# A down projection with sixteen of its 22 row tiles as seven block products

## The chip, the cores and the metric

The kernel runs on one core of one Trainium2 chip. The metric is the device time of one execution in microseconds, as the median of several runs. The engines are TensorE (PE: matmuls; PEld are its weight loads), VectorE (DVE), ScalarE (ACT), GpSimd (POOL) and SyncE (SP), whose queue issues most of the transfers.

## What is computed

A transformer block: modulation and norm, an input projection, two mixers (a chunkwise mLSTM and a block attention), a gated merge, and a gated feed-forward part. The end is what matters here (512 tokens, D = 1024, D_FF = 2816, all in float32):

```python
h = modulate(rms_norm(x, norm2_g[l]), sh2, sc2)
f = silu(h @ w_gate) * (h @ w_up)          # 512 x 2816
x = x + g2[:, None, :] * (f @ w_down)      # 2816 x 1024
return rms_norm(x, normf_g)
```

## The kernel before, in words

Every large matmul is made of float32r parts. A float32 operand is rounded to a "hi" part (ACT, line 207 for weights, 230 in `split` for activations) and the remainder "lo" is formed by a subtraction (DVE, lines 209 and 231). `mm3` (lines 223 to 227) then issues three matmuls: hi x hi, hi x lo, lo x hi.

Weights come in chunks of up to 128 x 2048 elements (1 MB). `load` issues a chunk's transfer on SP's queue into one of four `raw` tiles; `cvt` splits half a chunk into two of the four `whl` slots. `begin(n)` issues loads two and three chunks ahead and splits the first half of chunk n+1, `mid(n)` its second half. So a chunk's split can start only when the chunk two before it has been used up by PE and has given its slots back. The order on every engine is the order of the program; each engine works its own queue in order and waits on semaphores.

The feed-forward part has 22 gate and up chunks of 256 columns (C_GU to C_DN-1). From chunk FIRST = C_GU+3 to LAST, `seven` (line 1481) forms each by seven block products instead of eight; the block sums are made on DVE. The result f stands transposed in 22 tiles `ft[k]` of 128 rows by 512 tokens: the first sixteen in the pool `hp` (sixteen 128x512 tiles), the last six in the pool `xp`. Meanwhile the residual x is put aside in DRAM (`xkeep`, line 1591) and fetched back into `t` tiles before the down projection (line 1613). POOL forms the row sums of the gate g2 (`ada_sum`, lines 274 and 277) in the background of this stage, in bursts, on weights that use the same four `raw` tiles.

The down projection (lines 1619 to 1645) keeps eight PSUM banks open, one for each of four token blocks i and two column halves q. w_down comes in eleven chunks of 256 rows by 1024 columns. `gate_weights` (line 183) multiplies a chunk by the row g2 on DVE, four 128x512 operations for each chunk, so that PSUM holds the gated product. For each of the 22 k tiles, 4 x 2 `mm3` follow, that is 24 matmuls of 128x512; the stationary operand is f, the moving one is the weights. `fsplit(k+2)` splits the f tile two k tiles ahead. The last two chunks (four k tiles) are worked by `tail` in an order of banks that lets the last norm and the stores start early: first chunk NC-2 for a few banks ahead (`ahead_of`), then chunk NC-1 for one bank after the other, and `residual`, `root`, `close` and `scale` finish each token block.

## Time and profile before

| | |
|---|---|
| median of 3 runs | 775.61 us (775.3 to 776.21) |
| span of the profiled execution | 773.8 us |
| mean granted TensorE clock | 0.997 |
| instructions | 12047 |
| moved by DMA | 106.81 MB |

No time of the profiled execution other than its span is given, so the span stands for it. "Busy" is the time in which an engine executes; an operation's own duration includes a latency that the next one can overlap. A row of a group gives line, engine, operation, tiles written and read, shapes and count, then busy us, mean ns of one, and the idle time before it with what ended it. A row in order of time gives start, duration, engine, line, operation. Matmul rows overlap, so their rate is read from their starts.

### The profile page before, as it was taken

To read this page: it belongs to the slowest core of one execution; us is meant where nothing else is said; L and a number is where in the kernel's file an instruction comes from. 1 tells how busy PE (TensorE), PEld (TensorE's weight loads), DVE (VectorE), ACT (ScalarE), POOL (GpSimd) and SP (SyncE) were. 2 spreads that over 40 slices of the span, in tenths; PEclk is the share of its full clock that TensorE was granted. 3 is DMA by queue.
4 is the path that set the end of the run, shared out by engine and by line. 5 is a ranking of instruction groups with operands and counts; after the bars stand their busy time and mean duration, and the time that the engine had idled before them with its cause. 6 is when DMAs were issued, how large, how long until landed. Compare 5 with 4: busy or idle time off the path is not lost.

```text
span 773.8 us, 12047 instructions
## 1 busy us (share of the span) xinstructions
PE 762.4 (99%) x4635; PEld 665.3 (86%) x4635; DVE 543.9 (70%) x873; ACT 368.7 (48%) x656; POOL 328.2 (42%) x423
## 2 busy tenths in 40 slices
PE   8999999999999999999999999999999999999996
PEld 7789988778877877788889999999999998888885
DVE  5677877665575553388646789898999887754565
ACT  6679744323444553422347655545554543333143
POOL 5484535999875678980001108090835000000000
PEclk9999999999999999999999999999999999999998
DMA  9944325345421332327332522406053337422002
GB/s 333 389 167 179 110 81 161 106 169 218 163 111 55 110 118 109 155 97 284 109 109 89 178 75 91 183 25 231 32 219 152 122 114 240 135 84 108 1 1 108
DMA packets 25273, 106.81 MB, mean 138 GB/s; under 512 B 3704, under 2 KB 3840, under 8 KB 15616
## 3 DMA queue, kind: packets, MB, share of 16 engines
q1 hardware_dynamic: 23392, 103.62, 37.1%
q10 hardware_dynamic: 1824, 2.43, 1.2%
q8 instruction: 36, 0.59, 0.3%
q14 instruction: 21, 0.17, 0.1%
HBM read 99.74 MB, written 4.19 MB: 134 GB/s over the span
## 4 chain that ended last, share of the span: by engine, by line
PE 91%; DVE 5%; DMA 2%; ACT 1%; issue 1%; DVEq 0%; SPq 0%
PE psm L224 13%; PE psm L226 13%; PE psm L225 13%; PE psb L224 7%; PE psb L226 7%; PE psb L225 7%; PE psa L224 6%; PE psa L225 6%; PE psa L226 5%; PE psa L594 1%; DMA t<-in_dram 1%; PE psa L1095 1%; PE psc L1153 1%; PE psm L594 1%; PE psb L1136 1%; DVE whl L1452 1%
## 5 line engine op out<-in xcount | busy, mean ns | idle before, releaser
L209 DVE TENSOR_TENSOR whl<-raw,whl 128x1024 fp32r<-128x1024 f32 (+2 forms) x88 | 111.4, 1270 | 81.8 <-ACT whl L207 79.1
L207 ACT CAST whl<-raw 128x1024 fp32r<-128x1024 f32 (+2 forms) x87 | 88.5, 1033 | 104.1 <-PE psb L225 68.6
L277 POOL TENSOR_TENSOR accp<-accp,prod 128x256 f32<-128x256 f32 x112 | 97.9, 874 | 9.3
L274 POOL TENSOR_SCALAR prod<-ada,cact 128x256 f32<-128x256 f32 x112 | 93.0, 830 | 0.0
L1446 ACT CAST whl<-raw 128x1024 fp32r<-128x1024 f32 x57 | 59.8, 1049 | 69.0 <-DVE raw L1436 46.2
L1452 DVE TENSOR_TENSOR whl<-raw,whl 128x1024 fp32r<-128x1024 f32 x57 | 72.4, 1272 | 13.4 <-ACT whl L1446 13.2
L224 PE MATMUL psa<-t,whl 128*128 128x256 f32 x276 | 79.0, 286 | 0.9 <-DVE hs L1539 0.5
L226 PE MATMUL psa<-t,whl 128*128 128x256 f32 x276 | 78.1, 283 | 0.0
L225 PE MATMUL psa<-t,whl 128*128 128x256 f32 x276 | 78.1, 283 | 0.0
L224 PE MATMUL psm<-hh,whl 128*128 128x512 f32 x192 | 77.5, 404 | 0.5 <-ACT x L1077 0.5
L224 PE MATMUL psm<-t,whl 128*128 128x256 f32 (+1 forms) x256 | 76.1, 297 | 0.0
L225 PE MATMUL psm<-t,whl 128*128 128x256 f32 (+1 forms) x256 | 75.8, 296 | 0.0
L226 PE MATMUL psm<-t,whl 128*128 128x256 f32 (+1 forms) x256 | 75.8, 296 | 0.0
L226 PE MATMUL psm<-hh,whl 128*128 128x512 f32 x192 | 75.0, 390 | 0.0
L225 PE MATMUL psm<-hl,whl 128*128 128x512 f32 x192 | 74.9, 390 | 0.0
L1666 POOL TENSOR_TENSOR t<-t,t 128x512 f32<-128x512 f32 x1 | 1.3, 1293 | 170.2 <-DVE ss L1673 170.2
L224 PEld LDWEIGHTS psa<-t,whl 128*128 128x128 f32 x276 | 52.9, 192 | 1.6 <-DVE hs L1539 1.1
L225 PEld LDWEIGHTS psa<-t,whl 128*128 128x128 f32 x276 | 52.9, 192 | 0.1
L226 PEld LDWEIGHTS psa<-t,whl 128*128 128x128 f32 x276 | 52.9, 192 | 0.0
L225 PEld LDWEIGHTS psm<-t,whl 128*128 128x128 f32 x256 | 49.0, 191 | 1.3
L224 PEld LDWEIGHTS psm<-t,whl 128*128 128x128 f32 x256 | 49.0, 191 | 1.3
L226 PEld LDWEIGHTS psm<-t,whl 128*128 128x128 f32 x256 | 49.0, 191 | 1.3
(454 smaller groups left out, 2027.8 us busy)
## 6 DMA issues: line engine op xcount, KB each, us to landing
raw<-in_dram SPq DMA_DIRECT2D x59, 1024.0 KB, 4.8
ada<-in_dram SPq DMA_DIRECT2D x16, 1024.0 KB, 4.8
t<-in_dram SPq DMA_DIRECT2D x32, 256.0 KB, 6.0
raw<-in_dram SPq DMA_DIRECT2D x8, 448.0 KB, 6.3
xin<-in_dram SPq DMA_DIRECT2D x4, 512.0 KB, 5.5
t<-t ACTq DMA_DIRECT2D x32, 64.0 KB, 2.6
x<-in_dram SPq DMA_DIRECT2D x8, 256.0 KB, 7.0
xk<-x SPq DMA_DIRECT2D x8, 256.0 KB, 6.4
```

The costliest lines, as they stand in the source:

```text
L207: (eng.tensor_copy if eng else A.copy)(hi[:, s], raws[n][:, s])
L209: (eng or V).tensor_tensor(out=lo[:, s], in0=raws[n][:, s], in1=hi[:, s].bitcast(F32), op=ALU.subtract)
L224: PE.matmul(o, lh, rh, start=start, stop=False, skip_group_check=again)
L225: PE.matmul(o, lh, rl, start=False, stop=False, skip_group_check=again)
L226: PE.matmul(o, ll, rh, start=False, stop=stop, skip_group_check=again)
L274: G.tensor_scalar(t[:], rv[:, k, :], cact[:, k:k + 1], 1.0, op0=ALU.mult, op1=ALU.mult)
L277: G.tensor_tensor(out=p[:], in0=p[:], in1=t[:], op=ALU.add)
L594: PE.matmul(g1[m][:], w[:, blk(m)], h[:], start=k == 0 and e == 0, stop=k == KD - 1 and e == 2)
L1095: PE.matmul(bs[e][:, o:o + n], qp[a][r, blk(i)], kp[b][r, :n], start=g == 0, stop=g == 2)
L1136: PE.transpose(tb[:, o + (i - j) * 128:o + (i - j + 1) * 128], es[i][:, blk(j)], ident[:])
L1446: A.copy(hi, src)
L1452: V.tensor_tensor(out=lo, in0=src, in1=hi.bitcast(F32), op=ALU.subtract)
```

## The change

Sixteen k tiles (rows 512 to 2559 of w_down, `ft[4]` to `ft[19]`) leave the plain loop. They are taken as a product of 2 x 2 blocks: f in two token halves of 256 and two row halves of 1024, w_down in two row halves and two column halves of 512. Seven products (order 1, 2, 5, 6, 3, 7, 4) of 256 x 1024 by 1024 x 512 replace eight. Each product has two groups of four k tiles and two token blocks; its PSUM banks (`yb`, `xb2`, `zb`) hold on to partial results, which are copied out (`keep`) and combined later.

The four weight sums that the products need are formed in DRAM: POOL issues eight transfers of 2 MB (a copy, then an adding transfer, for each sum), the first two beside the merge projection (`next(wsums)` at ci = 0 and 2), the others before every third `seven`. `load` reads them as chunks. The f sums are formed in place in `ft`'s tiles, now four `hp` tiles of 128x2048: `sum3` on POOL, `sum1`, `sum2`, `sum4` on DVE. The products' weights are not gated by g2; `gated_sum` adds a kept tile to a PSUM bank on DVE, multiplies by g2 on POOL and adds to the residual on POOL. Three chunks stay plain (PLAIN: `ft` 0 to 3, 20, 21), of which the last two go to `tail`; the first one is gated on POOL. f's plain tiles are split one k tile ahead. The stores to `xkeep` move ahead of the first gate and up matmuls, and the first four f tiles lie in `xp`.

```diff
+PLAIN = (0, 1, 10)
...
-    for q in range(NF // 2):
+    for r in range(2):
+        for c in range(2):
+            for g in range(2):
+                got.append(("w_down", 512 + 1024 * r + 512 * g, 4, 512 * c, 512))
+    for q in PLAIN:
         got.append(("w_down", 256 * q, 2, 0, D))
...
+C_PL = 71
+PRODUCTS = (1, 2, 5, 6, 3, 7, 4)
...
-    hp = ctx.enter_context(tc.tile_pool(name="hp", bufs=16))
+    hp = ctx.enter_context(tc.tile_pool(name="hp", bufs=4))
...
+    def weight_sums():
+        for p, q, b in ((5, None, (0, 0)), (7, None, (1, 1)), (6, 7, (0, 0)), (4, 6, (1, 0))):
+            G.dma_start(wsum[p][:], wsum[q][:] if q else weight_block(0, 1), max_dma_last_dim=8192)
+            yield
+            G.dma_start(wsum[p][:], weight_block(*b), accum_op=ALU.add, max_dma_last_dim=8192)
+            yield
...
     xkeep = [dp.tile([128, D], F32, tag="xk", name=nm("xk")) for _ in range(NT)]
+    for i in range(NT):
+        for q in range(2):
+            SP.dma_start(xkeep[i][:, q * 512:q * 512 + 512], xr[i][q][:])
...
+    def aparts(t):
+        o, g, j = t // 4, t // 2 % 2, t % 2
+        b = {1: (0, 0), 2: (0, 1), 4: (1, 1), 7: (0, 0)}.get(PRODUCTS[o], (1, 0))
+        v = fblock(*b, g)[:, 2 * j:2 * j + 2, :]
+        ap[t] = tuple(T(dt=F32R)[:].rearrange("p (k t) -> p k t", k=2) for _ in range(2))
+        split(*ap[t], v)
+
+    def sum3(g, eng):
+        eng.tensor_tensor(out=fblock(0, 0, g), in0=fblock(0, 0, g), in1=fblock(1, 0, g), op=ALU.subtract)
...
     for n in range(FIRST, LAST + 1):
         if n == FIRST + 1:
             rows_free.append(1)
+        if (n - FIRST) % 3 == 0:
+            next(wsums, None)
         seven(n)
...
+    def gated_sum(name, banks, e, i, q, op):
+        t = kept[name][e]
+        V.tensor_tensor(out=t, in0=banks[e][:], in1=t, op=ALU.add)
+        G.tensor_tensor(out=t, in0=t, in1=g2row[q][:, :512], op=ALU.mult)
+        G.tensor_tensor(out=xr[i][q][:], in0=xr[i][q][:], in1=t, op=op)
...
+    hooks = {
+        (1, 0): lambda: sum3(1, G),
+        (2, 0): lambda: (keep("m1", yb, [W()[:, :512] for _ in range(2)]), sum1(0)),
+        (3, 0): lambda: sum1(1),
+        (4, 0): lambda: sum2(0),
+        (5, 0): lambda: sum2(1),
+        (6, 0): lambda: (keep("m5", zb, pair()), sum4(0)),
+        (7, 0): lambda: sum4(1),
+        (8, 0): lambda: keep("u2", yb, pair()),
+        (8, 1): lambda: gated_sum("m1", xb2, 0, 0, 0, ALU.add),
+        (9, 0): lambda: gated_sum("m1", xb2, 1, 1, 0, ALU.add),
+        (10, 0): lambda: gated_sum("u2", zb, 0, 0, 1, ALU.subtract),
+        (10, 1): lambda: gated_sum("u2", zb, 1, 1, 1, ALU.subtract),
+        (11, 1): lambda: gated_sum("m5", yb, 0, 2, 1, ALU.subtract),
+        (12, 0): lambda: (gated_sum("m5", yb, 1, 3, 1, ALU.subtract),
+                          gate_weights(C_PL, 0, G), gate_weights(C_PL, 1, G)),
+    }
+
+    groups = 2 * len(PRODUCTS)
+    for g in range(groups):
+        n = C_DN + g
+        p = PRODUCTS[g // 2]
+        for e in (2, 3):
+            load(n + e)
+        wh, wl = parts_of(n)
+        for e in range(2):
+            hooks.get((g, e), lambda: None)()
+            if g < groups - 1:
+                aparts(2 * g + 2 + e)
+            elif e == 0:
+                fps[0] = fsplit(0)
+            cvt(n + 1, e)
+            for k in range(4):
+                ah, al = (v[:, k % 2, blk(e)] for v in ap[2 * g + k // 2])
+                mm3(target[p][e][:], ah, al, wh[:, k, :], wl[:, k, :], p in (1, 2, 5) and g % 2 == 0 and k == 0,
+                    g % 2 == 1 and k == 3, True)
...
+    for e in range(2):
+        t = T()
+        V.tensor_tensor(out=t[:], in0=yb[e][:], in1=g2row[0][:, :512], op=ALU.mult)
+        G.tensor_tensor(out=xr[2 + e][0][:], in0=xr[2 + e][0][:], in1=t[:], op=ALU.add)
...
+    ch = begin(C_PL)
+    for kk in range(2):
+        if kk:
+            mid(C_PL)
+        fps[kk + 1] = fsplit(kk + 1)
...
+    last = [begin(C_PL + NP - 2)]
+    mid(C_PL + NP - 2)
+    last.append(begin(C_PL + NP - 1))
+    for k in range(3, 2 * NP):
+        fps[k] = fsplit(k)
```

## The prediction

> **What bounds the kernel now.** I read the page first (span, busy shares, chain), then the table by stage, then the groups and the order of time in the down projection.

> ```profile
> span 773.8 us, 12047 instructions
> PE 762.4 (99%) x4635; PEld 665.3 (86%) x4635; DVE 543.9 (70%) x873; ACT 368.7 (48%) x656; POOL 328.2 (42%) x423
> PE 91%; DVE 5%; DMA 2%; ACT 1%; issue 1%; DVEq 0%; SPq 0%
> ```

> TensorE is busy for 99% of the span and 91% of the chain that ended last runs through it. So a matmul taken away is worth its time, as long as nothing else becomes late. The table by stage says how much room the others have (columns: stretch, its length, then busy time and count of PE, PEld, DVE, ACT, POOL, then clock, DMA share, GB/s):

> ```profile
> 455.00:647.00 192.00, 191.14 (x1582) 190.30 (x1581) 173.32 (x240) 97.41 (x158) 72.69 (x60) 1.00 0.38 138
> 645.00:745.00 100.00, 99.87 (x449) 82.70 (x448) 60.90 (x84) 30.50 (x40) 0.00 (x0) 1.00 0.25 92
> 745.00:774.00 29.00, 22.32 (x110) 18.78 (x108) 17.46 (x47) 11.64 (x28) 1.29 (x1) 0.92 0.20 73
> ```

> The second row is the down projection: PE full, DVE at 61%, POOL idle. This is the stage that the change rebuilds. What one matmul costs there is read from the order of time: between these two rows lie one k tile's 24 matmuls.

> ```profile
> 739.81 0.39 PE L224 MATMUL psa<-whl,t 128*128 128x512 f32 x1
> ...
> 745.25 0.39 PE L224 MATMUL psa<-whl,t 128*128 128x512 f32 x1
> ```

> (745.25 - 739.81) / 24 = 0.2267 us each; the 0.39 is a latency, not a rate.

> **What goes.** Sixteen k tiles took 16 x 24 = 384 matmuls. Seven products of 2 token blocks x 8 k tiles x 3 parts are 336, of the same 128x512 form. 48 x 0.2267 = **10.9 us** less PE. Eight of eleven gated weight chunks also lose their four 128x512 multiplications on DVE. That ends a short stall just after the stage's start at 646.88, where PE's next start comes 0.52 instead of 0.23 us after the one before (a pause of 0.3):

> ```profile
> 646.88 0.40 PE L224 MATMUL psa<-whl,t 128*128 128x512 f32 x1
> ...
> 650.08 0.39 PE L226 MATMUL psm<-whl,t 128*128 128x512 f32 x1
> 650.60 0.50 PE L224 MATMUL psm<-whl,t 128*128 128x512 f32 x1
> ```

> **What is added beside PE.** The work is now 14 groups of 24 matmuls, 5.44 us each, and every group needs a whole new weight tile of 128x2048 rounded and subtracted; before, that fell on 48 matmuls, 10.9 us. The prices:

> ```profile
> L209 DVE TENSOR_TENSOR whl<-raw,whl 128x1024 fp32r<-128x1024 f32 x22 | 26.8, 1222 | 40.0 <-ACT whl L207 40.0
> L207 ACT CAST whl<-raw 128x1024 fp32r<-128x1024 f32 x22 | 23.0, 1049 | 72.0 <-PE psb L225 52.8 <-DVE raw L183 12.8 <-issue 6.3
> L231 DVE TENSOR_TENSOR t<-hs,t 128x512 fp32r<-128x512 f32 x16 | 11.0, 685 | 0.0
> L230 ACT CAST t<-hs 128x512 fp32r<-128x512 f32 x16 | 9.8, 615 | 0.0
> L1700 DVE SCALAR_TENSOR_TENSOR t<-t,ss,t 128x512 f32<-128x512 f32 x6 | 4.3, 749 | 0.1
> L1666 POOL TENSOR_TENSOR t<-t,t 128x512 f32<-128x512 f32 x1 | 1.3, 1293 | 170.2 <-DVE ss L1673 170.2
> ```

> These means hold some 0.09 us of latency; back to back DVE starts faster:

> ```profile
> 659.29 1.22 DVE L209 TENSOR_TENSOR whl<-raw,whl 128x1024 fp32r<-128x1024 f32 x1 [1.12 <-ACT whl L207]
> 660.44 1.29 DVE L183 TENSOR_TENSOR raw<-raw,v 128x512 f32<-128x512 f32 x2
> 661.64 0.68 DVE L231 TENSOR_TENSOR t<-hs,t 128x512 fp32r<-128x512 f32 x1
> 662.25 1.22 DVE L209 TENSOR_TENSOR whl<-raw,whl 128x1024 fp32r<-128x1024 f32 x1
> ```

> So 1.14 us for 1024 elements and 0.60 for 512; for ACT, the same way, 0.96 and 0.53. A group costs DVE 2 x 1.14 (weights) + 2 x 0.60 (f parts) = 3.5 us; in groups 2 to 7 an f sum of 1.14 to 1.24 comes on top: 4.7 of 5.44. ACT has 2 x 0.96 + 2 x 0.53 = 3.0. The weights of group n+1 can only be rounded when group n-1 has given its slots back, that is, from the start of group n, but then they need about 1.05 + 1.14 + 0.60 + 1.14 = 3.9 us of the 5.44. With DVE for itself, groups 0 to 13 keep PE full. I price them at zero, and DVE's 0.8 us of slack per group is the cover.

> **Where the cover goes.** POOL was idle here. Now it gets two 128x1024 subtractions (groups 0 and 1), then from group 8 six gated sums of two operations each, then the four multiplications that gate the first plain chunk, all 128x512 with both inputs in SBUF, and DVE runs the same kind. What the two do to each other stands in the old kernel's early stage:

> ```profile
> 77.22 1.23 DVE L209 TENSOR_TENSOR whl<-raw,whl 128x1024 fp32r<-128x1024 f32 x1 [1.23 <-ACT whl L207]
> 77.96 1.63 POOL L679 TENSOR_TENSOR t<-t,t 128x509 f32<-128x509 f32 x1 [1.21 <-ACT t L668]
> 78.37 1.77 DVE L647 SCALAR_TENSOR_TENSOR x<-t,t 128x512 f32<-128x512 f32 x1
> ```

> ```profile
> 558.19 1.59 POOL L277 TENSOR_TENSOR accp<-accp,prod 128x256 f32<-128x256 f32 x1
> 559.10 1.22 DVE L1452 TENSOR_TENSOR whl<-t,whl 128x512 fp32r<-128x512 f32 x1
> ```

> POOL's operation comes at 77.96, while DVE's is running; it gets on only when that ends (78.37), and DVE's next, which takes 0.749 alone (L1700), takes 1.77. They take turns, and POOL's waiting operation goes ahead of DVE's next. POOL ends at 79.59, 1.22 after its turn came; DVE ends 0.55 after that, so its turn began some 0.14 to 0.20 before POOL's end, and one POOL operation holds DVE up by 1.22 - 0.14 = **1.1 us**. The later pair of rows shows the same at half the size. [...]

> Laid on one time axis from the start of group 0 (group g at 5.44 g, the plain chunk at 76.2), each operation starting when its engine, its inputs, its slots and that access are free:
> First, groups 0 to 8: DVE has the slack for two double holds of 2.2; nothing is late.
> Second, groups 9 to 13. POOL's first gated sum comes at 47.5 (group 8 at 43.5, then 0.53 + 0.53 + 0.96 on ACT, 1.14 + 0.60 on DVE, 0.2 of latencies). Until the first half of the plain chunk's weights is ready, DVE still has 5 additions from PSUM at 0.60, 10 f remainders at 0.60 and 10 weight remainders at 1.14, 20.4 us. Ahead of it are 12 + 2 POOL operations; one of the 14 falls into a wait of DVE, 13 x 1.1 = 14.3. 47.5 + 20.4 + 14.3 = 82.2, against 76.2. Operation by operation, with ACT's waits, it is 82.5: PE is **6.3 us** late at the plain chunk.
> Third, the plain chunk's first half, 5.44 us of PE. From 82.5, DVE waits for POOL's last gate and ACT's rounding (1.1 + 0.2 + 1.05), then does the second weight half (1.14), two additions (1.2), two gates (1.2) with two more POOL operations between (2.2), waits for ACT (1.05), does a weight half (1.14), two gates (1.2), and only then the f remainder of k tile 1 (0.6): 82.5 + 12.1 = 94.6 (94.4 in the layout). PE wants that at 82.5 + 5.44 + 0.45 = 88.4. **6.1 us** with the half microsecond of latencies. Without POOL's turns both terms shrink to 0.7.
> Fourth, the tail. Before, f parts were split two k tiles ahead; now one ahead, so k tile 3 of the plain part is split after the last chunk's weights, whose slots come free when the plain chunk ends. Before, the same spot looked like this:

> ```profile
> 745.27 2.00 ACT L207 CAST whl<-raw 128x1024 fp32r<-128x1024 f32 x2 [6.33 <-issue]
> 746.36 2.36 DVE L209 TENSOR_TENSOR whl<-raw,whl 128x1024 fp32r<-128x1024 f32 x2 [4.91 <-ACT whl L207]
> 747.18 1.13 ACT L230 CAST t<-x 128x512 fp32r<-128x512 f32 x2
> 748.63 1.29 DVE L231 TENSOR_TENSOR t<-x,t 128x512 fp32r<-128x512 f32 x2
> ```

> There the first remainder was ready at 748.63 + 0.69 = 749.3, 4.1 us after the chunk's end at 745.25, and PE came to it then. Now PE wants it after 0.68 + 0.45 = 1.1: **3.0 us**, whatever POOL does.

> **The gate and up stage.** POOL issues eight 2 MB transfers from DRAM to DRAM, four of them adding. No row shows one. The nearest is 1 MB into SBUF in 4.8 us (the second row is for the stores below):

> ```profile
> raw<-in_dram SPq DMA_DIRECT2D x59, 1024.0 KB, 4.8
> ...
> xk<-x SPq DMA_DIRECT2D x8, 256.0 KB, 6.4
> ```

> The sums are needed stages later, so only others can suffer: weight loads that wait for POOL's row sums, and DVE behind them.

> ```profile
> SPq L163 <- POOL prod L274: 65.5, 4, 17.5
> ```

> ```profile
> DVE t L1431 <- DMA raw<-in_dram: 2.6, 3, 1.3
> ```

> Three loads already come late for DVE, yet DVE has 192 - 173 = 19 us free there. Below zero is excluded, since nothing is taken away; above, three loads later by a landing each, 3 x 4.8 = 14, less what DVE absorbs, about 6. I take **1.0**, nearest to the 2.6 now absorbed, range 0 to 6. [...] The eight stores to xkeep go ahead of one weight load on SP's queue, and the first f tiles wait for them; both have the second norm's projections as cover, and the larger tiles are given back with the same last readers: zero, at most one store's 6.4 us if the cover is gone.

> **Sum.** The profiled execution's span is 773.8; the median of the runs is 775.6, so 1.8 lie around it. 773.8 - 10.9 - 0.3 + 6.3 + 6.1 + 3.0 + 1.0 = 779.0, with 1.8 **780.8 us**, slower by 0.7%. Measurements of this kernel tell about 0.2% (1.6 us) from no change.

> **Rivals.** A: as above, 62%, 776 to 786 (the whole-instruction hold of 1.29 gives 784.1 and has some 10 of the 62; a DVE lead kept longer gives 776).
> B: POOL's operations do not hold DVE up in this stage, because they slip into DVE's waits for ACT (40.0 us before L209 in the old stage). Then the stall is 0.7 + 3.0: 775.6 - 10.9 - 0.3 + 3.7 + 1.0 = 769.1. For it speaks that idle time; against it, that DVE's load per time doubles and that idle time shrinks to 0.8 us per group. It decides where POOL's total hold from group 8 on, 16 x 1.1 = 18 us, fits DVE's gaps. 18%.
> C: half of the holds fall into gaps: laid out with 0.65 per hold, 8 us of stall: 773.3, range 771 to 777. 12%.
> D: the transfers starve the weight loads, at the far end, 6 instead of 1: 785.8 to 788. It takes over where a load lands over 3 us late in two of the bursts. 8%.
> That the matmuls saved are not saved can't be; their count and form are written out.

> Faster by over 0.2% (below 774.1): B and 7 of C's 12, 25%. Slower by over 0.2% (above 777.2): 55 of A, 8 of D, 63%. Same: 12%. The range for eight in ten, 769 to 787, cuts half of B and half of D; A's own is 776 to 786.

> **What would show it.** Right: PE full to about group 10, then pauses of PE that ACT's and DVE's weight groups end; POOL's 128x512 operations at some 1.9 to 2.4 us instead of 1.29 from group 8 on; L209 and L231 longer than 1.22 and 0.685 there; a wait of ACT's rounding for POOL's gates; a pause of 3 us just after the plain chunk, ended by an f remainder on DVE. The down projection still starts within 2 us of 646.88. Wrong: POOL rows near 1.3 with DVE rows unchanged (B), or PE waits before the down projection behind weight loads (D).

## The result, and the profile after

The changed kernel takes 786.94 us (median of four runs, 786.13 to 787.13), the kernel before 775.82 us beside it (775.3 to 776.21): a ratio of 1.0137, 95% interval 1.0125 to 1.015. It is slower, by 11.1 us, where the prediction had said slower by 5.2. The direction and the mechanism stand; the size is twice the forecast's.

First the page of the changed kernel: span, busy time of each engine, and the chain that ended last.

```profile
span 785.3 us, 12061 instructions
PE 761.3 (97%) x4587; PEld 660.2 (84%) x4587; DVE 576.5 (73%) x875; ACT 390.0 (50%) x686; POOL 370.0 (47%) x451
PE 84%; DVE 7%; DMA 4%; POOL 2%; issue 2%; ACT 1%; SPq 0%; ACTq 0%; POOLq 0%; DVEq 0%
```

The 48 matmuls are gone (4635 to 4587), but PE's busy time fell by only 1.1 us, not by 10.9. So something made the remaining matmuls longer, and PE's share of the chain fell from 91% to 84%. The table by stage shows where (columns: stretch, length, busy time and count of PE, PEld, DVE, ACT, POOL, then granted clock, DMA share, GB/s):

```profile
653.00:700.00 47.00, 46.70 (x204) 37.62 (x203) 42.10 (x43) 29.34 (x41) 6.26 (x3) 1.00 0.51 182
700.00:730.00 30.00, 24.70 (x103) 19.06 (x103) 29.71 (x22) 11.16 (x15) 24.88 (x14) 0.99 0.44 158
730.00:745.00 15.00, 11.07 (x40) 8.32 (x40) 11.22 (x12) 2.86 (x4) 6.07 (x4) 0.84 0.00 0
745.00:760.00 15.00, 12.46 (x37) 9.24 (x36) 7.91 (x11) 6.61 (x9) 0.00 (x0) 0.73 0.00 0
```

Up to 700 us (about group 9) PE is full. From there to 730, in groups 9 to 13, DVE is busy for 29.7 of 30 us and PE for 24.7: DVE is the bound. Behind that DVE has room again, but PE is still not full, and the granted clock is at 0.84 and 0.73. The kernel before had 1.00 in its whole down projection.

Why DVE is full stands in the groups of 700 to 730 us (out<-in, shape, count, then busy time and mean ns of one), and in those of POOL from 690 to 735:

```profile
L253 DVE TENSOR_TENSOR whl<-raw,whl 128x1024 fp32r<-128x1024 f32 x8 | 16.3, 2036 | 0.0
L275 DVE TENSOR_TENSOR t<-f,t 128x512 fp32r<-128x512 f32 x8 | 10.2, 1278 | 0.0
```

```profile
L1690 POOL TENSOR_TENSOR t<-t,t 128x512 f32<-128x512 f32 x4 | 8.6, 2156 | 0.3
L227 POOL TENSOR_TENSOR raw<-raw,v 128x512 f32<-128x512 f32 x4 | 7.9, 1991 | 0.0
L1689 POOL TENSOR_TENSOR t<-t,v 128x512 f32<-128x512 f32 x4 | 6.9, 1715 | 4.7 <-DVE t L1688 4.7
```

The weights' remainder (L253) takes 2.04 us where it took 1.22, the f remainder (L275) 1.28 where it took 0.685; POOL's operations take 1.7 to 2.2 instead of 1.29. Both engines pay for the other. In order of time the turns look like this:

```profile
696.97 1.67 POOL L1689 TENSOR_TENSOR v<-v,v 128x512 f32<-128x512 f32 x1 [38.85 <-DVE v L1688]
697.41 2.31 DVE L253 TENSOR_TENSOR whl<-raw,whl 128x1024 fp32r<-128x1024 f32 x1
698.72 2.16 POOL L1690 TENSOR_TENSOR t<-t,v 128x512 f32<-128x512 f32 x1
699.65 0.68 DVE L1688 TENSOR_TENSOR v<-psm,v 128x512 f32<-128x512 f32 x1
700.25 1.18 DVE L275 TENSOR_TENSOR t<-f,t 128x512 fp32r<-128x512 f32 x1
```

DVE's weight remainder is held by 1.1 us, its f remainder by 0.5; the addition between them (L1688), which has one of its inputs in PSUM, keeps 0.68 although POOL's second operation runs beside it. From 697 to 732 us fifteen of DVE's operations last 14.0 us longer in all than they do alone; the prediction had 14.3 for this stretch.

What PE and ACT waited for (in all, times, longest):

```profile
PE psa L269 <- DVE whl L253: 5.5, 5, 2.1
PE psa L268 <- ACT t L274: 3.9, 2, 2.1
PE psa L270 <- DVE t L275: 2.6, 2, 1.8
ACT whl L251 <- POOL raw L227: 11.1, 2, 8.2
```

In order of time, the pauses of PE beyond one matmul's spacing are 1.21, 1.81, 0.67 and 2.27 us in groups 10 to 13, each ended by DVE's weight remainder; 2.28 and 1.98 at the second half of the first plain chunk; 1.90 and 0.97 in the tail, ended by ACT's and DVE's part of k tile 3. The chain that ended last shows how the first two lead to the third (start, length, what):

```profile
725.22 7.87 POOL raw L227 x4
733.11 1.06 ACT whl L251
734.20 1.22 DVE whl L253
735.42 1.20 DVE t L1736 x2
736.62 3.02 DVE raw L227 x2
739.80 1.05 ACT whl L251
740.88 1.22 DVE whl L253
742.10 1.21 DVE raw L227 x2
743.31 0.61 DVE t L275
743.96 0.79 PE psa L270
```

POOL's four gates, then ACT, DVE, two more gates (stretched from 1.3 to 3.0 by POOL's last additions), ACT, DVE again, and only then a 0.6 us f remainder that needs none of all this but stands behind it in DVE's list.

So far this is the forecast. The part that it lacks is in the clock. The clock record changes only at points 3.41 us apart; cut at these, the table reads:

```profile
712.25:715.66 3.41, 1.77 (x8) 1.42 (x8) 3.41 (x3) 1.31 (x2) 2.70 (x2) 1.00 0.21 38
725.90:729.32 3.42, 1.31 (x6) 1.05 (x6) 3.42 (x2) 0.12 (x1) 3.42 (x3) 1.00 0.02 7
729.32:732.73 3.41, 3.41 (x9) 2.64 (x8) 2.05 (x2) 0.93 (x1) 3.41 (x2) 0.50 0.02 5
739.56:742.97 3.41, 0.73 (x2) 0.30 (x2) 2.17 (x4) 1.56 (x2) 0.00 (x0) 1.00 0.00 0
742.97:746.38 3.41, 2.42 (x6) 1.94 (x7) 2.30 (x5) 1.23 (x2) 0.00 (x0) 0.50 0.00 0
746.38:749.80 3.42, 3.42 (x10) 2.65 (x9) 2.87 (x4) 1.82 (x3) 0.00 (x0) 0.50 0.00 0
753.21:756.62 3.41, 1.43 (x5) 0.91 (x6) 3.41 (x5) 2.17 (x4) 0.00 (x0) 1.00 0.00 0
756.62:760.04 3.42, 3.42 (x10) 2.64 (x9) 1.05 (x2) 0.00 (x0) 0.00 (x0) 0.50 0.00 0
```

The first window, with PE busy for 1.77 us, is followed by full clock (8 matmuls start in it). The three with 1.31, 0.73 and 1.43 are followed by 0.50, and there 9 or 10 matmuls fill a window that takes 15 at full clock (3.41 / 0.2267). The stretches at half clock cost PE 1.6, 2.5 and 1.6 us, worked out from the spacing of the matmuls in them (0.43 instead of 0.2267).

### The profile page after: what moved, and what is told of

Read it like the earlier page. It is cut to its first block, busy times and chain, and to the rows that moved or that the text cites. A ratio compares the mean times of both kernels' runs of the same rounds, so it can differ in the third digit from the quotient of the medians.

```text
span 785.3 us, 12061 instructions
## 1 busy us (share of the span) xinstructions
PE 761.3 (97%) x4587; PEld 660.2 (84%) x4587; DVE 576.5 (73%) x875; ACT 390.0 (50%) x686; POOL 370.0 (47%) x451
## 4 chain that ended last, share of the span: by engine, by line
PE 84%; DVE 7%; DMA 4%; POOL 2%; issue 2%; ACT 1%; SPq 0%; ACTq 0%; POOLq 0%; DVEq 0%
PE psm L268 13%; PE psm L269 12%; PE psm L270 12%; PE psb L268 7%; PE psb L269 7%; PE psb L270 7%; PE psa L270 5%; PE psa L268 5%; PE psa L269 5%; DMA raw<-in_dram 2%; PE psa L638 1%; DMA t<-in_dram 1%; DVE whl L1489 1%; PE psa L1139 1%; PE psc L1197 1%
## 5 line engine op out<-in xcount | busy, mean ns | idle before, releaser
L253 DVE TENSOR_TENSOR whl<-raw,whl 128x1024 fp32r<-128x1024 f32 (+2 forms) x100 | 133.5, 1339 | 50.9 <-ACT whl L251 48.2
L251 ACT CAST whl<-raw 128x1024 fp32r<-128x1024 f32 (+2 forms) x99 | 101.0, 1036 | 79.9 <-PE psb L269 19.5
L1483 ACT CAST whl<-raw 128x1024 fp32r<-128x1024 f32 x57 | 59.8, 1049 | 68.7 <-DVE raw L1473 41.8
L318 POOL TENSOR_SCALAR prod<-ada,cact 128x256 f32<-128x256 f32 x112 | 89.5, 799 | 0.1
L268 PE MATMUL psm<-hh,whl 128*128 128x512 f32 x192 | 77.5, 404 | 0.5 <-ACT x L1121 0.5
L270 PE MATMUL psm<-hh,whl 128*128 128x512 f32 x192 | 74.9, 390 | 0.0
L269 PE MATMUL psm<-hh,whl 128*128 128x512 f32 x192 | 74.9, 390 | 0.0
L318 POOL TENSOR_SCALAR accp<-ada,cact 128x256 f32<-128x256 f32 x16 | 10.7, 671 | 87.6 <-DMA ada<-in_dram 87.6
## 6 DMA issues: line engine op xcount, KB each, us to landing
raw<-in_dram SPq DMA_DIRECT2D x57, 1024.0 KB, 4.8
ada<-in_dram SPq DMA_DIRECT2D x16, 1024.0 KB, 4.8
ws<-in_dram POOLq DMA_DIRECT2D x6, 2048.0 KB, 14.3
t<-in_dram SPq DMA_DIRECT2D x32, 256.0 KB, 5.8
raw<-ws SPq DMA_DIRECT2D x8, 1024.0 KB, 4.9
```

The costliest lines, as they stand in the source:

```text
L251: (eng.tensor_copy if eng else A.copy)(hi[:, s], raws[n][:, s])
L253: (eng or V).tensor_tensor(out=lo[:, s], in0=raws[n][:, s], in1=hi[:, s].bitcast(F32), op=ALU.subtract)
L268: PE.matmul(o, lh, rh, start=start, stop=False, skip_group_check=again)
L269: PE.matmul(o, lh, rl, start=False, stop=False, skip_group_check=again)
L270: PE.matmul(o, ll, rh, start=False, stop=stop, skip_group_check=again)
L318: G.tensor_scalar(t[:], rv[:, k, :], cact[:, k:k + 1], 1.0, op0=ALU.mult, op1=ALU.mult)
```

## The experiments

All times are medians; the kernel before ran beside each and had 775.75 to 776.23. T1 is the theory above: turns between GpSimd (POOL) and VectorE (DVE), and half clock behind the pauses that they cause. R1: the transfers. R2: VectorE's list is too long by itself, and GpSimd merely late. R3: the half clock has another cause, or costs nothing.

**One split earlier (e1).**

```
     root_table()
+    fps[3] = fsplit(3)
     last = [begin(C_PL + NP - 2)]
...
-    for k in range(3, 2 * NP):
+    for k in range(4, 2 * NP):
```

> Only the place of one split changes: row tile 3 of the plain part is split before the last chunk's weights are rounded, not behind them. T1 (pauses of PE, and half clock in the window behind a long pause): in the changed kernel the tail waited 1.90 us for ScalarE's part and 0.97 us for VectorE's part of this split; both go, and with them the half-clock stretch of 3.41 us that followed at 756.62 (1.7 us): 786.9 - 2.9 - 1.7 = 782.3, between 781.5 and 783.5. R3 (the half clock has nothing to do with the pauses): only the pauses go, 784.0. R1 (transfers set the end): no change, 786 to 787.

Measured: 781.71 us (ratio to before 1.0077, 1.0062 to 1.0092), 5.2 less than the changed kernel. Both pauses of the tail are gone, and so is the half clock behind them; no other long pause moves by more than 0.1 us. Moving one split ahead of two weight halves is worth 5.2: 2.9 of pauses, 1.6 of half clock, and 0.7 that these two don't account for. R1's "no change" falls here, and so does R3 as far as the half clock behind this pause goes.

**GpSimd without its gated sums (e3), and with fills in their place (e4).**

```
         V.tensor_tensor(out=t, in0=banks[e][:], in1=t, op=ALU.add)
-        G.tensor_tensor(out=t, in0=t, in1=g2row[q][:, :512], op=ALU.mult)
-        G.tensor_tensor(out=xr[i][q][:], in0=xr[i][q][:], in1=t, op=op)
+        for _ in range(2):              # e4 only
+            G.memset(t, 0.0)
```

> Leaves out of the computation the gating and the adding of six product sums (GpSimd's two operations each; VectorE's additions stay). T1 (GpSimd's operations and VectorE's take turns): the pauses of groups 10 to 13 (1.21, 1.81, 0.67, 2.27 us) go, VectorE's rounding of weights is back at 1.22 us in these groups, and since GpSimd then gates the first plain chunk earlier, most of the 4.3 us at that chunk goes too; with them two of the three half-clock stretches (1.7 and 3.4 us): 774 to 778. R2 (GpSimd is merely late, and VectorE's list of work in these groups is too long by itself): the pauses of groups 10 to 13 stay, and only the plain chunk's and its half clock go: 779 to 781. R1: 786.

> As the kernel without GpSimd's gating and adding (the same part of the computation is left out), but with two fills of the same 128x512 tile in the place of the two operations, so GpSimd writes and reads nothing. T1 with turns taken for operands that are read: VectorE's operations keep their time alone (1.22 and 0.69 us), 774 to 778, like the kernel without. T1 with turns for any operation of GpSimd: as much is lost as GpSimd's fills last; at 1.3 us each the pauses stay, 784 to 787. R2: 779 to 781.

Measured: 772.53 us without (771.94 to 773.63), 777.28 with fills. In both, the pauses of groups 10 to 13 are gone: PE is busy for 30.00 of the 30 us from 700 to 730 (first row without, second with fills), though VectorE does all its own work:

```profile
700.00:730.00 30.00, 30.00 (x133) 24.56 (x132) 25.70 (x26) 13.35 (x18) 10.34 (x6) 1.00 0.43 156
700.00:730.00 30.00, 30.00 (x135) 24.81 (x133) 26.81 (x26) 11.84 (x16) 14.56 (x14) 1.00 0.42 153
```

So R2 falls. The fills show what it is in GpSimd's operations that holds VectorE up. From the order of time of the kernel with fills, VectorE and GpSimd:

```profile
696.16 0.68 DVE L275 TENSOR_TENSOR t<-f,t 128x512 fp32r<-128x512 f32 x1
696.31 1.12 POOL L1690 MEMSET v<- 128x512 f32 x2 [38.86 <-DVE v L1688]
696.76 1.22 DVE L253 TENSOR_TENSOR whl<-raw,whl 128x1024 fp32r<-128x1024 f32 x1
```

Two fills lie across two of VectorE's operations, and all keep their time alone (0.68, 1.22; a fill 0.53). Here GpSimd's fills, which read nothing from SBUF, held neither of them.

The kernel without landed below its range, because with GpSimd free its gates of the plain chunk came early, and none of its windows fell low enough for half clock (the clock is at 1.00 from 700 to 760 us). The kernel with fills spread over its runs, from 774.36 at a mean clock of 0.996 to 778.97 at 0.990; its profiled run, the fastest, had one window at half clock. Only that run has a trace; that in the slower ones the pauses at the plain chunk empty more windows, since the grid lies elsewhere, is the author's estimate from their lower mean clock and not shown.

**No weight sums (e5).** The operands of all products are read from plain blocks, and the eight transfers are not issued.

> Leaves out of the computation the four weight sums: no accumulating transfers, and the seven products read the plain weight blocks in their place (as many loads of the same size). T1: only the later start of the down projection goes (648.11 against 646.88 before), so 1.2 us: 785.7, between 785 and 786.5; its pauses stay. R1 (transfers hold back loads or weight loads of PE in the down projection): 782 or less, with shorter pauses there.

Measured: 785.35 us, 1.6 less than the changed kernel. The down projection starts at 646.47 instead of 648.11, and its pauses in groups 10 to 13 are 1.21, 1.80, 0.72 and 2.26, the same as with the sums. The price of forming the sums by transfers is this 1.6, in the stages before.

Behind the stage's start the half clock fell otherwise than in the changed kernel: none at 729, then 738.62 to 745.45 and 752.27 to 759.10. Yet PE came to the matmul that waits for the plain chunk's f remainder 95.87 us after the stage's start, against 95.85, since the pause ahead of the chunk's second half was 3.81 instead of 2.28: without the half clock at 729, PE waited that much longer. Behind that, this kernel's half clock costs it 1.3 us less up to the end of the tail's pauses and 1.2 more from there on; that the two cancel is chance. The prediction's rival D (785.8 to 788) had come closest to the result, for a reason that isn't there.

**The plain chunk's gates on VectorE (e2).**

```
-                          gate_weights(C_PL, 0, G), gate_weights(C_PL, 1, G)),
+                          gate_weights(C_PL, 0), gate_weights(C_PL, 1)),
```

> The first plain chunk's four gating operations on VectorE, not on GpSimd. In the changed kernel GpSimd's four lasted from 725.22 to 733.08 and ScalarE's rounding waited 2.87 us behind the last. T1 with the chain GpSimd, ScalarE, VectorE setting the end there: VectorE does 4 x 0.69 = 2.8 us more and gets back about 3.2 us that its own operations then lasted longer; the chain loses some 2 to 4 us: 782 to 785. R3 (the lost time is PE's half clock, set by something else): no change, 786 to 788.

Measured: 781.41 us (1.006 to 1.009 of before), 5.5 less, for giving VectorE 2.8 us more to do, and a little more than expected (782 to 785). Group 13's pause grew from 2.27 to 3.24 us, the plain chunk's fell from 4.26 to 1.63, and of the half clock only that of the tail is left. The longest pause had no half clock behind it: it lay across two windows.

**Matmuls that keep PE busy (e7, e7b).** In e7b, 8 and 9 matmuls with a stationary of zeros accumulate into a bank in use:

```
+        if kk:
+            filler(8, db[0][1][:])
...
+                filler(FILL.pop((e, i, kk), 0), db[i][q][:, o:o + w])    # 9, ahead of the tail's k tile 3
```

> Adds 56 matmuls that change nothing in the result (into a free bank; at the plain chunk and the tail with a stationary of zeros), put where PE paused: 5, 8, 3 and 10 in groups 10 to 13, 18 ahead of the plain chunk's second half and 12 in the tail, 12.7 us of matmuls in all. T1: the clock stays at 1.0 up to the end, and although work is added the time falls by up to 6.8 us; since VectorE and GpSimd set when the next operands are there, part comes back as waiting: 780 to 785. R3 (half clock has another cause than the pauses): the half-clock stretches stay, 787 to 790, as the added matmuls fill the pauses at best.

> The first kernel with added matmuls held back the last weights: its fillers in the tail read a tile in the slot that these weights need (VectorE's rounding started 1.9 us after ScalarE's), and the 18 ahead of the plain chunk's second half outlasted the pause. Here 8 fillers lie ahead of that half and 9 ahead of the tail's second row tile, with a stationary of zeros and the split f tile as moving operand. T1': the half clock at 729.32 is covered, since GpSimd, VectorE and ScalarE set the time up to 743.96; those of 743.96 to 749.80 (2.9 us) and of 756.62 to 760.04 (1.7 us) are not: 4.6 us less, 782.3, if both go, between 781.5 and 784. R3' (PE at full clock only waits longer, so that no half clock costs anything): 786 to 787.5.

Measured: 785.88 us for the first, which missed both ranges. Its clock did stay at 1.00 from 729 to 757 us, but its fillers in the tail delayed the last weights, as the second's expectation tells. The second has 783.28 us, 3.7 less than the changed kernel although PE does 17 matmuls more: the window at 756.62 is at full clock, of the two from 742.97 on one is left. In both the clock was at 1.00 at 729, and PE's wait for the plain chunk's f remainder still ended at 744.41 and 743.59 (743.96 in the changed kernel). So the first half clock cost next to nothing: there PE had to wait anyway, as the kernel without sums shows too. R3' falls for the other two, which e7b took away in part.

**Pauses where there were none (e8).** GpSimd copies a tile between two matmuls that read it, once in each of groups 1 to 7, with growing length:

```
+                if e == 1 and k == 2 and g in held:
+                    PE.matmul(spare[:], probe[g][:, :128], probe[g][:], ...)
+                    hold(g, held[g])
+                    PE.matmul(spare[:], probe[g][:, :128], probe[g][:], ...)
```

> Adds seven pauses of growing length (some 0.5 to 4 us) to groups 1 to 7, where PE is otherwise full and the clock stayed at 1.00: PE waits for GpSimd to copy a tile of which TensorE has just read the old content. Nothing else is changed there. Law read from the six traces so far: the clock is set on a fixed grid of 3.41 us; a window at full clock with PE busy up to 37% is followed by half clock, one with 39% or more is not, whatever engine caused the pause. T1 so expects half clock behind each window that the longer pauses (from about 2.1 us, if they fall into one window) empty below 38%, and none behind the short ones, in a place where the changed kernel had none. R3 (the half clock comes from what the end of the down projection does): clock 1.00 through groups 1 to 9.

Measured (one run, 807.86 us): PE paused for 1.65, 1.32, 1.42, 2.22, 1.60, 3.82 and 2.26 us. By windows of the grid, around the fourth, sixth and seventh:

```profile
680.98:684.39 3.41, 1.35 (x7) 0.81 (x6) 2.88 (x3) 0.00 (x0) 2.07 (x3) 1.00 0.42 139
684.39:687.80 3.41, 3.41 (x9) 2.63 (x9) 0.00 (x0) 0.77 (x1) 0.30 (x1) 0.50 0.40 168
698.04:701.46 3.42, 1.56 (x7) 0.94 (x6) 3.42 (x4) 1.33 (x2) 1.73 (x2) 1.00 0.14 17
701.46:704.87 3.41, 1.61 (x7) 1.35 (x8) 1.48 (x2) 0.00 (x0) 1.68 (x2) 1.00 0.75 293
704.87:708.28 3.41, 3.41 (x17) 2.82 (x16) 2.20 (x3) 2.90 (x4) 0.00 (x0) 1.00 0.02 5
708.28:711.70 3.42, 1.32 (x7) 0.78 (x6) 0.76 (x1) 0.21 (x1) 1.85 (x3) 1.00 0.44 110
711.70:715.11 3.41, 3.41 (x9) 2.63 (x10) 0.00 (x0) 0.28 (x1) 0.00 (x0) 0.50 0.47 197
```

The pauses of 2.22 and 2.26 us, each within one window, are followed by half clock; the one of 3.82 us, spread over two, is not; the short ones are not. The expectation's limit of 37 to 39% counts what the matmuls streamed, while the busy time in these rows holds their latency too; by matmuls streamed the four windows with a pause have 5.3, 6.1, 6.6 and 5.1 of 15, and only those with 5.3 and 5.1 are followed by half clock. R3 falls: here pauses alone brought the half clock, in a stretch that had none.

**GpSimd's second operation as a transfer (e10), with e1 and e2 besides (e6).**

```
-        V.tensor_tensor(out=t, in0=banks[e][:], in1=t, op=ALU.add)
+        if op == ALU.add:
+            V.tensor_tensor(out=t, in0=banks[e][:], in1=t, op=ALU.add)
+        else:
+            V.scalar_tensor_tensor(out=t, in0=banks[e][:], scalar=-1.0, in1=t, op0=ALU.mult, op1=ALU.subtract)
         G.tensor_tensor(out=t, in0=t, in1=g2row[q][:, :512], op=ALU.mult)
-        G.tensor_tensor(out=xr[i][q][:], in0=xr[i][q][:], in1=t, op=op)
+        G.dma_start(xr[i][q][:], t, accum_op=ALU.add)
```

> The changed kernel with nothing but GpSimd's second operation of the six gated sums turned into an accumulating transfer. T1: with six turns of 1.1 us fewer, pauses of 6.0 us in groups 10 to 13 fall by 4 to 6; the plain chunk's wait for GpSimd's gates begins that much earlier and stays as long, the tail's 2.9 us and its half clock stay: 780 to 783. R2: 785 or more, as VectorE's own list is unchanged.

> GpSimd's second operation of each of the six gated sums becomes an accumulating transfer of 256 KB from GpSimd's queue into the residual tile (VectorE forms the sum with its sign); the first plain chunk's gating is on VectorE, and row tile 3 is split early. T1: six turns of 1.1 us and the chain at the plain chunk go: from 781.7 for the early split some 5 us of pauses in groups 10 to 13, 2 to 3 us at the plain chunk and 1.7 to 2.9 us of half clock: 770 to 775, beside 775.8 for the kernel before. R1 (accumulating transfers are themselves what costs): 778 or more. R2 (VectorE's list is too long by itself): 776 to 779.

Measured: 780.42 and 771.87 us. The first is in T1's range by its sum, but not by its place: the pauses in groups 11 and 13 are 1.05 and 4.37 us, hardly shorter in all than the 5.96 of the changed kernel, since GpSimd's gates now come in group 13; what became shorter is the plain chunk's wait, 1.61 instead of 4.26. The half clock now lies behind group 13's pause (725.88 to 732.71); the tail's pauses of 1.90 and 0.97 stayed, but the window that holds most of the first kept 6.2 matmuls, and no half clock followed there. The second is faster than the kernel before (0.9949, 0.9934 to 0.9964). Its pauses are 1.07, 1.35 and 1.63 us, and the clock is at 1.00 up to the end of the matmuls.

**Spread, and then without GpSimd's arithmetic (e9, e11).** e9 is e6 with the gated sums of product 1 in groups 4 and 6 and f tiles 1 to 3 split earlier. e11 adds to that:

```
-        G.tensor_tensor(out=t, in0=t, in1=g2row[q][:, :512], op=ALU.mult)
+        V.tensor_tensor(out=t, in0=t, in1=g2row[q][:, :512], op=ALU.mult)
...
-        G.tensor_tensor(out=xr[2 + e][0][:], in0=xr[2 + e][0][:], in1=t[:], op=ALU.add)
+        G.dma_start(xr[2 + e][0][:], t[:], accum_op=ALU.add)
```

> As the kernel with accumulating transfers (771.9), and besides: the sums of product 1 are gated in groups 4 and 6, not 8 and 9, the second of u2 in group 11, the plain chunk's gates stand in groups 12 and 13, and f row tile 1 is split in group 13, tiles 2 and 3 in the plain chunk. T1: of the 4.1 us of pauses left there (1.07, 1.35, 1.63 us) the last goes and the first two mostly: 768 to 770. R2 (VectorE's list of work from group 10 on is too long whatever the order): 770.5 to 772.

> As the spread kernel (770.4), but VectorE does the gating of the six sums itself, and the last two additions into the residual are accumulating transfers too, so GpSimd computes nothing from group 2 on and only issues transfers. T1: one operation of GpSimd held VectorE up by 1.1 us, more than the 0.6 us that VectorE takes for the same multiplication, so VectorE gets back 6 x 0.5 + 2 x 1.1 = 5 us from group 4 on, although it does six operations more; most of the 3.2 us of pauses left in the spread kernel go: 767 to 769.5. R2 (VectorE's list is the bound and what GpSimd takes over is a help): 771 to 774.

Measured: 770.44 us for e9, just outside T1's range: the pause that its early split was to take away came back ahead of the tail (1.58 us), since VectorE's list up to there was still full. At 770.44 it is also just short of R2's range (770.5 to 772), and its profiled run, the slowest of the five, has one window at half clock behind that pause. 767.63 us for e11 (0.9887, 0.9871 to 0.9904), the fastest of all. VectorE does six multiplications more than in e9, and yet its table row from 700 to 730 and its groups from 690 to 730 read:

```profile
700.00:730.00 30.00, 30.00 (x135) 24.82 (x134) 26.88 (x36) 14.57 (x19) 5.16 (x6) 1.00 0.70 199
```

```profile
L253 DVE TENSOR_TENSOR whl<-raw,whl 128x1024 fp32r<-128x1024 f32 x15 | 18.3, 1220 | 3.2 <-ACT whl L251 3.2
L275 DVE TENSOR_TENSOR t<-f,t 128x512 fp32r<-128x512 f32 x12 | 8.2, 686 | 1.0 <-ACT t L274 1.0
```

PE full, and every operation of VectorE back at its time alone, with some idle time in front. Beyond the waits of groups 1 and 2 only one pause of 0.5 us is left. e11 takes the six multiplications and two additions from GpSimd at once, so how its 2.8 us divide between them is open.

## Why the prediction went wrong, point by point

**The step that failed is the sum.** It counts each lateness of PE as a pause and every matmul at 0.2267 us, because the clock stood at 1.00 in the old down projection. With pauses in it, that no longer holds: the half clock behind them is a term of its own, and it was missing. Beside each other, in us of the profiled executions:

| term | forecast | measured | from |
|---|---|---|---|
| 48 matmuls less | -10.9 | -10.9 | counts |
| stall at the stage's start | -0.3 | 0 | that one is gone, but group 1 has one of 0.38 |
| groups 9 to 13 | +6.3 | +6.0 | 1.21 + 1.81 + 0.67 + 2.27 |
| first plain chunk | +6.1 | +5.9 | 2.28 + 1.98, and 1.6 of half clock that took the place of waiting |
| tail, k tile 3 | +3.0 | +2.9 | 1.90 + 0.97 |
| stages before | +1.0 | +1.2 | 646.88 to 648.11 |
| half clock, where PE was the bound | 0 | +4.1 | 2.5 + 1.6 |
| waits under 0.4 us, and what else is left | 0 | +2.3 | the rest |
| sum | +5.2 | +11.5 | 773.8 to 785.3 |

**Right: the hold.** 1.1 us for each POOL operation gave the two stalls in which POOL has a part to within 0.3 us, and the experiments with fills and without GpSimd show the cause. The access that the layout lets an operation wait for is its turn beside the other engine's. No run shows a hold of POOL's whole 1.29 us, which rival A's 784.1 takes: of DVE's operations from 697 to 730 us, those that one of POOL's held for a whole turn lasted 1.06 to 1.11 us longer (L253 2.28 to 2.33 instead of 1.22, L275 1.77 or 1.78 instead of 0.68). Rivals B and C, in which all or half of POOL's operations slip into DVE's waits, are out: DVE's operations lasted 14.0 us longer, of 14.3 forecast, and e3 shows what the stage looks like without most of these holds.

**Right: the tail.** It was priced as work in the wrong place of an in-order list, whatever POOL does, and e1 took it out alone.

**Too low, a little: the transfers.** 1.0 was taken, 1.2 measured in the trace and 1.6 by e5. No load in the down projection suffers: from 648 us on the loads into `raw` landed after 4.7 to 5.0 us (4.6 to 4.8 before), and no wait there is put down to one.

**Wrong: "groups 0 to 13 keep PE full" at a price of zero.** The 2.3 us are what the other rows leave over. In order of time, 1.9 us of them lie between matmuls that come late by less than 0.4 us each. Two kinds can be told apart. The matmul behind the one that ended a long pause came 0.34 us after it instead of 0.23, which makes 0.8 in all. And groups 1 and 2 have 1.1 us of such lateness (the stall of 0.38 in it), where the whole down projection before had 0.4. The rows show what stood in the way there:

```profile
649.11 2.39 POOL L1645 TENSOR_TENSOR f<-f 128x1024 f32<-128x1024 f32 x1 [53.20 <-DVE t L275]
649.28 2.77 DVE L1506 TENSOR_TENSOR x<-x,t 128x512 f32<-128x512 f32 x1
652.92 1.21 DVE L253 TENSOR_TENSOR whl<-raw,whl 128x1024 fp32r<-128x1024 f32 x1
654.18 0.50 PE L269 MATMUL psa<-whl,t 128*128 128x512 f32 x1 [0.21 <-DVE whl L253]
```

Beside POOL's first f subtraction a 128x512 operation of DVE took 2.77 us, where the f remainder of that size takes 0.68; DVE came to group 1's weights only at 652.92, and PE waited for them. The second subtraction did the same to group 2. The prediction had these two double holds, of the right size, and found slack for them. No experiment took them alone, so this rests on the trace: e11, which keeps both subtractions, has the same waits in groups 1 and 2 and none from 700 to 730 us.

**What the forecast could have seen.** The pauses that it laid out, some 6 us ahead of the plain chunk, 6 in it and 3 behind it, were long enough to empty windows. The profile of before has the matching row at its end, where the clock of 745 to 774 us is 0.92: it stands at 1.00 up to 769.34 us and at 0.50 from there to the end, and in the 3.41 us ahead of that PE is busy for only 1.39. In the changed kernel, too, PE was not idle in such a window, but busy for up to 1.43 us of 3.41, and in e8 a single pause of 2.22 us was enough.

## What to carry to other kernels

A pause of PE that left fewer than six matmuls of 128x512 in a 3.41 us window cost its own length here and then up to 1.6 us more per window at half clock, unless PE had to wait there anyway; short pauses, or one that lay across two windows, brought no half clock where each window kept more than that (6.1 and 6.6 in e8). Work given to GpSimd was no help to a full VectorE when both read two operands from SBUF: here one such operation cost VectorE 1.1 us and doing it itself 0.6, and beside accumulating transfers VectorE's operations kept their 1.22 and 0.69 us (e11). Where an engine works its list in order, look for the short operation that needs nothing and stands behind one that waits: one of them, moved, gave 5.2 us.
